# Operand tiles at other SBUF addresses, and reordered stage edges, in a hybrid two-layer decoder kernel

## The chip, the cores and the metric

One Trainium2 core of eight is used. The metric is the device time of one execution of the whole program in microseconds, median of several runs. The kernel before takes 1634.8 us (three runs: 1633.64, 1634.80, 1635.77).

The core has engines with a queue of instructions each: TensorE (PE, matrix products; PEld are its weight loads), VectorE (DVE), ScalarE (ACT), GpSimd (POOL), and SyncE (SP), which here only issues DMA transfers. Each engine works through its own queue in order; between engines order comes from semaphores. SBUF is the on-chip memory of 128 partitions, PSUM the accumulators of TensorE (eight banks of 128x512 fp32).

## The reference

A trunk of two layers on 512 tokens of width 1024, all in fp32:

```python
h = rms_norm(x, attn_norm[l])
proj = h @ w_in[l]                       # 5536 columns
gate_cols, mla_cols, rwkv_cols, conv_cols = split(proj)
o_a = mla_branch(mla_cols, ...)   @ mla_w_o[l]     # low-rank causal attention, 8 heads
o_b = rwkv7_branch(rwkv_cols, h, ...) @ rwkv_w_o[l]  # gated linear recurrence, 4 heads
o_c = short_conv_branch(conv_cols, ...) @ conv_w_o[l]
g = sigmoid(gate_cols).reshape(..., 3, 1024)
x = x + (g[0] * o_a + g[1] * o_b + g[2] * o_c) @ w_out[l]
h2 = rms_norm(x, mlp_norm[l])
x = x + square(relu(h2 @ w_up[l])) @ w_down[l]     # 1024 -> 4096 -> 1024
```

The recurrence of `rwkv7_branch` updates a 64x64 state per head and token; the kernel runs it in chunks of 64 tokens, each chunk as small matrix products.

## The kernel before, in words

**Layout.** Activations lie with channels on partitions and the 512 tokens along the free axis; a 128x512 tile is one slice of 128 channels. A dense product accumulates 128 output channels x 512 tokens in one PSUM bank over the slices k of its input.

**Three products for one.** Every fp32 operand of a dense product is split into hi (rounded) and lo (the rest), and each slice takes three matmuls with a 128x128 weight and a 128x512 moving operand: hi·act_hi (L269), hi·act_lo (L271), lo·act_hi (L273), in `gemm_steps`. Weights stream from DRAM in blocks of 128x512: `load_weights` issues the DMA into a `raw` tile (three buffers, L242), ScalarE casts it to `hi` (L243), VectorE subtracts to `lo` (L244), four buffers each. One block serves twelve matmuls. An input slice x is split in the same way into `xg` tiles: hi by ScalarE (L296), lo by VectorE (L297).

**Order.** TensorE's order is that of the program text (the matmuls stand under a manual schedule). The other engines' queues are ordered by a scheduler that simulates a timeline, with a few operations raised by `high_priority`. Because the recurrence and the attention are chains of small operations, the program weaves dense matmuls in between: `independent()` yields, matmul by matmul, the gate products and others that need only `xg`; `fill(n)` takes n of them, with the counts in the table `FC`.

**Stages of one layer.** (1) Norm of the input and five tiles of the input projection, one output tile after another; `normed_steps` (L309, sums of squares over channels) and `normed_spread` (L322–L324: four copies and transposes that spread the factor over partitions into `rstd`) are woven in; the first evacuations `col<-pg,rstd` wait for `rstd`. (2) The rest of the RWKV columns. (3) Chunk inputs: for each half j of the width, a chain on VectorE (cumulated decay L671, `k2` L673/L675, `a_` L676, `eC` L682, `ex` L685, `kk` L691, the four products into `ar` L696–L702), with exponentials on ScalarE (L679, L681), then `fill(FC["am"])` dense matmuls, then the products `pa,pb<-ar,ar` on TensorE (L714). (4) The recurrence over eight chunks; each has a group of 64x64 products at L842, in a loop over the output pair p and inside it over h. (5) Attention. (6) Merge: for each m of eight output tiles, load a gate tile `z` from DRAM (L1168), the product of `oa` (L1169, moving tile `prep`), gate and add (L561, L1170), split into hi and lo (L1174, L1175); then the product with `w_out` (moving tiles `ar` and `mix`), L1184. (7) MLP in four quarters q: eight up tiles (moving `xg`), then eight down tiles (192 matmuls) whose moving operands are the tiles `us` made from the up tiles: hi in `mix`, lo in `prep` for even q; hi in `ar`, lo in `mg` for odd q.

**Where the tiles lie.** All tiles come from one pool `sb`, which places tags in the order in which they first appear. Read from the compiled program, in bytes of each partition:

| tag | before | after |
|---|---|---|
| weights hi, lo | 29,792–46,175 | 7,264–23,647 |
| xg | 46,176–78,943 | 23,648–56,415 |
| prep | 101,472–122,271 | 56,416–76,895 |
| mix | 144,000–160,383 | 76,896–93,279 |
| ar | 162,464–178,847 | 93,280–109,663 |
| mg | 178,848–201,727 | 109,664–132,191 |
| raw | 23,648–29,791 | from 148,576 |

Of the kernel before, what the change touches and what calls it, by code (L numbers as in the profile page):

```python
# [16 lines left out]
F32R = mybir.dt.float32r  # L17
# [23 lines left out]
FC = {"ss": 9, "pk": 16, "am": 42, "tri0": 6, "tri1": 10, "join0": 22, "join1": 9, "join2": 8, "in1": 9, "py": 2,  # L41
# [16 lines left out]
def _blocks(inp, l):  # L58
# [3 lines left out]
    for t in RW_ORDER[:3]:  # L62
        out.append(_cols(w_in[:, r0 + t * P:r0 + (t + 1) * P]))
# [4 lines left out]
    out.append(_cols(ex))  # L68
# [98 lines left out]
def trunk(tc, w, wkv, wq, xin, pos, pp, sm, rg, out, sizes):  # L167
# [4 lines left out]
    const = es.enter_context(tc.tile_pool(name="const", bufs=1))  # L172
    sb = es.enter_context(tc.tile_pool(name="sb", bufs=1))
# [4 lines left out]
    BUFS = {"xg": 16, "mix": 8, "prep": 10, "am": 1, "ar": 4, "inv": 9, "tok": 2, "raw": 3, "hl": 4, "z": 2,  # L178
            "mg": 11, "col": 7, "g": 2, "a": 2, "b": 2, "c": 2}
    cnt = [0]  # L180

    def tl(tag, shape=(P, T), dt=F32, bufs=None):
        cnt[0] += 1
        if tag in ("prep", "mg") and tuple(shape) == (P, T):
            return sb.tile([P, 520 if tag == "prep" else T + 2], dt, tag=tag, name=f"{tag}_{cnt[0]}", bufs=BUFS[tag])[:, 0:T]
        return sb.tile(list(shape), dt, tag=tag, name=f"{tag}_{cnt[0]}", bufs=bufs or BUFS[tag])

# [99 lines left out]
    def split(tag, src, scale=None, tag_lo=None):  # L287

        hi = tl(tag, (P, T), F32R)
        lo = tl(tag_lo or tag, (P, T), F32R)  # L290
        if scale is None:
            A.copy(hi, src)
            V.tensor_tensor(out=lo, in0=src, in1=hi, op=ALU.subtract)
        else:
            last_split[:] = [
                A.activation(out=hi, in_=src, func=AF.Copy, scale=scale),  # L296
                V.scalar_tensor_tensor(out=lo, in0=src, scalar=scale, in1=hi, op0=ALU.mult, op1=ALU.subtract)]  # L297
        return hi, lo

# [192 lines left out]
    for l in range(NL):  # L492
        pr, dv, rgl = ppt[l], drv[l], rgt[l]
        sl = tl("sm", (P, 3 * RW), bufs=1)
        nc.sync.dma_start(out=sl, in_=sm[l])
# [67 lines left out]
        def independent():  # L563
# [103 lines left out]
        for j in range(2):  # L667
# [5 lines left out]
            V.tensor_scalar(out=k2, in0=a_, scalar1=dv[:, 6 + j:7 + j], scalar2=dv[:, 8 + j:9 + j],  # L673
                            op0=ALU.mult, op1=ALU.add)
            V.tensor_tensor(out=k2, in0=k2, in1=kt[j], op=ALU.mult)  # L675
            V.tensor_scalar(out=a_, in0=a_, scalar1=-0.5, scalar2=-0.5, op0=ALU.mult, op1=ALU.add)  # L676
            eW = tl("prep", (P, 8, C + 1))
# [7 lines left out]
            V.tensor_copy(ex, rs16v[:, :, j, :].unsqueeze(3).to_broadcast([P, NB, 2, C]))  # L685
# [20 lines left out]
            fill(FC["am"])  # L706
# [115 lines left out]
        def chunk_inputs(b):  # L822
# [17 lines left out]
            for p in range(2):  # L840
                for h, hs in enumerate(hss):
# [129 lines left out]
        def shared_key():  # L971
# [6 lines left out]
            kpr = tl("tok2", (P, NB, 32), bufs=1)  # L978
# [186 lines left out]
        for m in range(8):  # L1165
            wb = weights()
            z = tl("z")
            nc.sync.dma_start(out=z, in_=zd[l][:, m * T:(m + 1) * T])  # L1168
            run(branch_steps(z, wb, oa, 0, P, z))  # L1169
            (V if m > 5 else G).tensor_tensor(out=mg[m], in0=mg[m], in1=z, op=ALU.add)  # L1170
            if m % 2 == 0:
                mh = tl("ar", (P, 2, T), F32R)
            lo = tl("mix", (P, T), F32R)
            A.copy(mh[:, m % 2], mg[m])  # L1174
            V.tensor_tensor(out=lo, in0=mg[m], in1=mh[:, m % 2], op=ALU.subtract)  # L1175
            merged.append((mh[:, m % 2], lo))
# [17 lines left out]
        for q in range(4):  # L1194
            us = []
            for m in range(8):
# [49 lines left out]
```

## Time and profile before

| what | value |
|---|---|
| runs, median (lowest, highest) | 1634.8 us (1633.64, 1635.77) |
| profiled execution, its own time | 1636.34 us |
| its span, first to last instruction | 1634.6 us |
| TensorE busy | 1617.3 us, 99% |
| VectorE busy | 1016.8 us, 62% |
| ScalarE busy | 659.3 us, 40% |
| DMA | 156.79 MB, mean 96 GB/s |
| mean granted clock of TensorE | 0.998 |

A row of the timeline reads: start (us), duration (us), engine, line, operation, output<-inputs, shapes, count, and in brackets how long the engine sat idle before it and what released it. Matmuls are pipelined: the time that one occupies in the stream is the distance from its start to the next start, not its duration. In the view of windows a row is the stretch, its length, then for each engine the busy time with the number of instructions, then TensorE's granted clock (1.00 is full), the DMA engines' share and GB/s; asked for one engine, only that engine's column stands there.

### The profile page before, as it was taken

The page shows a single profiled execution, that of the slowest core. Times are in us where ns is not written, and L with a number is a line of the kernel's source. Part 1 is how long each engine was busy: PE and PEld are TensorE (multiplying, and loading weights), DVE is VectorE, ACT ScalarE, POOL GpSimd, SP SyncE. Part 2 cuts the span into 40 slices and gives each one's busy share as a digit, 9 for nine tenths or more (in the row PEclk, how much of TensorE's full clock was granted, in tenths as well). Part 3 has the DMA queues.
Part 4 walks back from the last instruction along what each step waited for, and adds up shares of the span by engine and source line. Part 5 has one row for each costly group of instructions (what it writes and reads, how often), then busy time and mean ns, then how long its engine had stood idle before and what let it go on. Part 6 is the DMA issues. An engine that isn't in the chain of part 4 may idle for free.

```text
span 1634.6 us, 22593 instructions
## 1 busy us (share of the span) xinstructions
PE 1617.3 (99%) x8126; PEld 1306.0 (80%) x8126; DVE 1016.8 (62%) x1988; ACT 659.3 (40%) x1457; POOL 185.8 (11%) x192
## 2 busy tenths in 40 slices
PE   8999999999999999999999999999999999999998
PEld 7878778877788888888887887887777888888887
DVE  7789577676754444544567886686766544444453
ACT  5332556454443232424333335654534433323241
POOL 1212024102100000000022121251120000000000
PEclk9999999999999999999999999999999999999999
DMA  5323322214323333333432243222143333333333
GB/s 163 95 73 108 110 66 80 82 46 129 123 91 97 97 97 95 95 95 97 141 98 78 79 127 92 63 72 73 51 146 113 92 95 97 97 97 96 93 96 103
DMA packets 85072, 156.79 MB, mean 96 GB/s; under 512 B 10080, under 2 KB 12384, under 8 KB 84448
## 3 DMA queue, kind: packets, MB, share of 16 engines
q1 hardware_dynamic: 84960, 155.35, 32.3%
q8 instruction: 64, 1.05, 0.3%
q14 instruction: 48, 0.39, 0.1%
HBM read 146.40 MB, written 8.91 MB: 95 GB/s over the span
## 4 chain that ended last, share of the span: by engine, by line
PE 93%; DVE 3%; DMA 2%; issue 1%; ACT 0%; SPq 0%; POOL 0%; DVEq 0%; ACTq 0%
PE pg L271 15%; PE pg L269 15%; PE pg L273 15%; PE pa L273 4%; PE pa L271 4%; PE pa L269 4%; PE pb L273 4%; PE pb L271 4%; PE pb L269 4%; PE pc L271 4%; PE pc L273 4%; PE pc L269 4%; PE pa L1115 2%; DMA z<-z_spill 1%; PE pc L1141 1%; DVE lo L244 1%
## 5 line engine op out<-in xcount | busy, mean ns | idle before, releaser
L243 ACT CAST hi<-raw 128x512 fp32r<-128x512 f32 (+1 forms) x499 | 307.1, 618 | 629.2 <-PE pg L271 255.6
L244 DVE TENSOR_TENSOR lo<-raw,hi 128x512 fp32r<-128x512 f32 (+1 forms) x499 | 358.2, 718 | 244.6 <-ACT hi L243 239.1
L269 PE MATMUL pg<-xg,hi 128*128 128x512 f32 x784 | 312.3, 398 | 2.9 <-ACT xg L296 2.2
L271 PE MATMUL pg<-xg,hi 128*128 128x512 f32 x784 | 313.8, 400 | 0.3 <-DVE xg L297 0.3
L273 PE MATMUL pg<-xg,lo 128*128 128x512 f32 x784 | 310.0, 395 | 0.0
L269 PEld LDWEIGHTS pg<-xg,hi 128*128 128x128 f32 x784 | 147.9, 189 | 39.3 <-issue 4.7
L271 PEld LDWEIGHTS pg<-xg,hi 128*128 128x128 f32 x784 | 148.0, 189 | 34.2 <-issue 5.8
L273 PEld LDWEIGHTS pg<-xg,lo 128*128 128x128 f32 x784 | 147.8, 189 | 31.6 <-issue 2.3
L303 POOL TENSOR_TENSOR t<-t,mhalf 128x4 f32<-128x4 f32 (+1 forms) x26 | 48.9, 1882 | 560.8 <-DVE t L314 536.7
L269 PE MATMUL pg<-ar,hi 128*128 128x512 f32 x192 | 75.7, 394 | 0.1
L273 PE MATMUL pg<-ar,lo 128*128 128x512 f32 x192 | 75.5, 393 | 0.0
L273 PE MATMUL pa<-xg,lo 128*128 128x512 f32 x160 | 62.6, 391 | 0.0
L269 PE MATMUL pa<-xg,hi 128*128 128x512 f32 x160 | 62.3, 390 | 0.0
L271 PE MATMUL pa<-xg,hi 128*128 128x512 f32 x160 | 62.3, 389 | 0.0
L271 PE MATMUL pg<-mix,hi 128*128 128x512 f32 x144 | 57.5, 399 | 1.3 <-DVE mix L1175 1.3
L273 PE MATMUL pb<-xg,lo 128*128 128x512 f32 x144 | 56.2, 390 | 0.0
L269 PE MATMUL pb<-xg,hi 128*128 128x512 f32 x144 | 56.1, 390 | 0.0
L271 PE MATMUL pb<-xg,hi 128*128 128x512 f32 x144 | 56.0, 389 | 0.0
L1119 ACT ACTIVATE inv<-pa,t 128x128 f32<-128x128 f32 (+3 forms) x64 | 33.7, 527 | 46.2 <-DVE t L1117 45.7
L271 PE MATMUL pg<-prep,hi 128*128 128x512 f32 x128 | 50.5, 394 | 0.0
L269 PE MATMUL pc<-xg,hi 128*128 128x512 f32 x128 | 50.0, 390 | 0.0
L273 PE MATMUL pc<-xg,lo 128*128 128x512 f32 x128 | 49.8, 389 | 0.0
(385 smaller groups left out, 3197.7 us busy)
## 6 DMA issues: line engine op xcount, KB each, us to landing
raw<-in_w_dram SPq DMA_DIRECT2D x493, 256.0 KB, 2.6
z_spill<-z SPq DMA_DIRECT2D x16, 256.0 KB, 3.1
z<-z_spill SPq DMA_DIRECT2D x16, 256.0 KB, 2.9
raw<-in_wq_dram SPq DMA_DIRECT2D x12, 192.0 KB, 2.3
am<-in_x_dram SPq DMA_DIRECT2D x8, 256.0 KB, 6.1
raw<-in_wkv_dram SPq DMA_DIRECT2D x8, 256.0 KB, 2.7
am<-in_x_dram SPq DMA_DIRECT2D x2, 1024.0 KB, 6.1
x_spill<-am SPq DMA_DIRECT2D x8, 256.0 KB, 2.9
```

Source lines behind the costliest of these rows:

```text
L243: A.copy(hi[:, c], raw[:, c])
L244: V.tensor_tensor(out=lo[:, c], in0=raw[:, c], in1=hi[:, c], op=ALU.subtract)
L269: mm(dst, hi[:, c0:c0 + P], ah, start=(k == 0), stop=False)
L271: mm(dst, hi[:, c0:c0 + P], al, start=False, stop=False)
L273: mm(dst, lo[:, c0:c0 + P], ah, start=False, stop=(k == n - 1))
L303: G.tensor_tensor(out=y, in0=v, in1=mhalf.to_broadcast([P, n]), op=ALU.pow)
L1115: mm(psc[:, 0:n], qT[hf][h // 2][0:HD, h % 2, b * P:n], kT[hf][h // 2][0:HD, h % 2, 0:n], start=True, stop=False)
L1119: A.activation(out=pe[:, 0:n], in_=psc[:, 0:n], func=AF.Exp, bias=nm[:, h:h + 1], accum_out=rsum[:, h:h + 1])
L1141: mm(po[halves[i], f], Vm[hf][kb // 2][:, kb % 2, 2 * f + i], pT[2 * f + i][:, kb * P:(kb + 1) * P], start=(kb == 0), stop=(kb == b))
```

## The change

1. A second pool `sbl`, allocated first, takes the tags hi, lo, xg, prep, mix, ar and mg, all with 2048 bytes per buffer (the padding to 520 and 514 columns is gone); the few odd-sized tiles go to `kql` and `rv`. The table above shows the addresses that result.
2. The first four tiles of the input projection (three RWKV tiles and the extra tile) are computed slice by slice: four accumulators are open, and for each k all four take their three matmuls. The host packs the weights accordingly, and the loads of x and of the weights alternate. `normed_steps` comes after all 96 matmuls, `normed_spread` inside the fifth tile.
3. `raw` has four buffers.
4. In the chunk chain, `k2`'s and `a_`'s scalings and the copies `eC` and `ex` move from VectorE to ScalarE, and `FC["am"]` becomes (50, 40) for j = 0, 1 instead of 42 for both.
5. The loop at L842 has h outside and p inside.
6. In the merge, `z` is loaded into `inv` (nine buffers) instead of `z` (two), and the last two additions and splits are raised in priority. `places` chooses the tiles of `merged` and of `us`: for m < 4 of even quarters `mix`, above it `prep`; for odd quarters `ar` and `mg`; for `merged`, `ar` and `mix`.

```diff
-FC = {"ss": 9, "pk": 16, "am": 42, ...
+FC = {"ss": 9, "pk": 16, "am": (50, 40), ...
...
+    sbl = es.enter_context(tc.tile_pool(name="sbl", bufs=1))
     sb = es.enter_context(tc.tile_pool(name="sb", bufs=1))
...
-    BUFS = {"xg": 16, ..., "raw": 3, "hl": 4, "z": 2,
+    BUFS = {"xg": 16, ..., "raw": 4, "hl": 4, "z": 2,
...
-        if tag in ("prep", "mg") and tuple(shape) == (P, T):
-            return sb.tile([P, 520 if tag == "prep" else T + 2], dt, tag=tag, ...)[:, 0:T]
-        return sb.tile(list(shape), dt, tag=tag, ...)
+        pool = sbl if tag in ("hi", "lo", "xg", "prep", "mix", "ar", "mg") else sb
+        return pool.tile(list(shape), dt, tag=tag, ...)
...
+    def places(m, tag):
+        if tag is None:
+            return tuple(tl("mix" if m < 4 else "prep", (P, T), F32R) for _ in range(2))
+        if m < 4:
+            both = tl("ar", (P, 2, T), F32R)
+            return both[:, 0], both[:, 1]
+        return tuple(tl(tag, (P, T), F32R) for _ in range(2))
+
+    def split_into(hl, src):
+        A.copy(hl[0], src)
+        V.tensor_tensor(out=hl[1], in0=src, in1=hl[0], op=ALU.subtract)
...
     for k in range(KD):
         nc.sync.dma_start(out=xt[:, k], in_=xin[:, k * T:(k + 1) * T])
-        if k in (0, 3):
-            ahead.append(load_weights(2))
-    ahead += [load_weights(2), load_weights()]
+        if k < 4:
+            ahead.append(load_weights(2 if k < 2 else 1))
...
-        pgs = []
-        at = 2 if l else 3
-        for i, pst in enumerate(("g", "g", "a", "b", "a")):
-            pgs.append(rwkv_gemm(pst, normed_steps if i == at else None))
-            if i == at:
+        pgs = [pt(pst) for pst in ("g", "g", "a", "b")]
+        for k, (ah, al) in enumerate(xg):
+            hi, lo = weights()
+            for t, pg in enumerate(pgs):
+                c = slice(t * P, (t + 1) * P)
+                mm(pg, hi[:, c], ah, start=(k == 0), stop=False)
+                mm(pg, hi[:, c], al, start=False, stop=False)
+                mm(pg, lo[:, c], ah, start=False, stop=(k == KD - 1))
+        for _ in normed_steps:
+            pass
+        pgs.append(pt("a"))
+        for i, _ in enumerate(gemm_steps(pgs[4], None, xg)):
+            if i == 14:
                 normed_spread()
...
-            V.tensor_scalar(out=k2, in0=a_, scalar1=dv[:, 6 + j:7 + j], scalar2=dv[:, 8 + j:9 + j],
-                            op0=ALU.mult, op1=ALU.add)
+            A.activation(out=k2, in_=a_, func=AF.Identity, scale=dv[:, 6 + j:7 + j], bias=dv[:, 8 + j:9 + j])
             V.tensor_tensor(out=k2, in0=k2, in1=kt[j], op=ALU.mult)
-            V.tensor_scalar(out=a_, in0=a_, scalar1=-0.5, scalar2=-0.5, op0=ALU.mult, op1=ALU.add)
+            A.activation(out=a_, in_=a_, func=AF.Copy, scale=-0.5, bias=-0.5)
...
-            V.tensor_copy(eC[:, j, :], eW[:, :, C])
+            A.copy(eC[:, j, :], eW[:, :, C])
...
-            V.tensor_copy(ex, rs16v[:, :, j, :].unsqueeze(3).to_broadcast([P, NB, 2, C]))
+            A.copy(ex, rs16v[:, :, j, :].unsqueeze(3).to_broadcast([P, NB, 2, C]))
...
-            fill(FC["am"])
+            fill(FC["am"][j])
...
-            for p in range(2):
-                for h, hs in enumerate(hss):
+            for h, hs in enumerate(hss):
+                for p in range(2):
                     mm(prs[p][halves[1 - p], hs], AM[halves[p], h, b, p, halves[1 - p]], uvs[p][halves[p], hs], ...)
...
-            z = tl("z")
+            z = tl("inv")
             nc.sync.dma_start(out=z, in_=zd[l][:, m * T:(m + 1) * T])
             run(branch_steps(z, wb, oa, 0, P, z))
-            (V if m > 5 else G).tensor_tensor(out=mg[m], in0=mg[m], in1=z, op=ALU.add)
-            ...
+            merged.append(places(m, "mix"))
+            with tc.high_priority() if m > 5 else nullcontext():
+                (V if m > 5 else G).tensor_tensor(out=mg[m], in0=mg[m], in1=z, op=ALU.add)
+                split_into(merged[m], mg[m])
...
-                if q % 2 == 0:
-                    us.append(split("mix", rl, tag_lo="prep"))
-                else:
-                    ...
+                us.append(places(m, "mg") if q % 2 else places(m, None))
+                split_into(us[m], rl)
```

**The start on TensorE.** The first dense matmuls of the program; `xg_138`, `xg_139` are hi and lo of slice k = 0, `xg_142`, `xg_143` those of k = 1, and `hi_99`, `hi_102` are weight blocks. Before:

```order
L215 MATMUL pc_81<-ident 128x128 x9
L269 MATMUL pg_323<-xg_138,hi_99 128x512
L271 MATMUL pg_323<-xg_139,hi_99 128x512
L273 MATMUL pg_323<-xg_138,lo_100 128x512
L269 MATMUL pg_323<-xg_142,hi_99 128x512
L271 MATMUL pg_323<-xg_143,hi_99 128x512
```

Of the change (the three matmuls of the loop stand at L544–L546 there):

```order
L544 MATMUL pg_321<-xg_138,hi_102 128x512
L545 MATMUL pg_321<-xg_139,hi_102 128x512
L546 MATMUL pg_321<-xg_138,lo_103 128x512
L544 MATMUL pg_322<-xg_138,hi_102 128x512
L545 MATMUL pg_322<-xg_139,hi_102 128x512
L546 MATMUL pg_322<-xg_138,lo_103 128x512
L544 MATMUL pa_323<-xg_138,hi_102 128x512
L545 MATMUL pa_323<-xg_139,hi_102 128x512
L546 MATMUL pa_323<-xg_138,lo_103 128x512
L544 MATMUL pb_324<-xg_138,hi_102 128x512
```

Slice k = 1 is needed after three matmuls before, after twelve now.

**The chunk chain on VectorE**, layer 0, up to the product `ar_812` that the L714 matmuls of j = 0 wait for (rows of j = 1 stand among them). Before:

```order
L685 COPY prep_923<-t_140_740 128x512
L244 TENSOR_TENSOR lo_935<-raw_933,hi_934 128x512
L675 TENSOR_TENSOR prep_914<-prep_914,mix_574 128x512
L676 TENSOR_SCALAR prep_756<-prep_756 128x512
L682 COPY eC_708<-prep_918 128x8
L700 TENSOR_TENSOR prep_809<-prep_809,prep_748 128x512
L732 SCALAR_TENSOR_TENSOR prep_762<-mix_522,pp_78,prep_762 128x512
L547 TENSOR_TENSOR col_847<-pg_796,rstd_322 128x512
L244 TENSOR_TENSOR lo_967<-raw_965,hi_966 128x512
L701 TENSOR_TENSOR ar_812<-prep_809,prep_760 128x4x128
```

Of the change:

```order
L724 TENSOR_TENSOR ar_812<-prep_762,prep_760 128x4x2x64
L697 TENSOR_TENSOR prep_931<-prep_931,mix_574 128x512
L722 TENSOR_TENSOR prep_809<-prep_809,prep_748 128x512
L246 TENSOR_TENSOR lo_891<-raw_889,hi_890 128x512
L754 SCALAR_TENSOR_TENSOR prep_762<-mix_522,pp_81,prep_762 128x512
L723 TENSOR_TENSOR ar_812<-prep_809,prep_760 128x4x128
L720 TENSOR_TENSOR ar_971<-mix_617,kql_935 128x4x2x64
L570 TENSOR_TENSOR col_847<-pg_796,rstd_320 128x512
```

L685, L676 and L682 are gone from this queue (L673, which stood four rows ahead of the first row shown, too), one `lo` (L244) fewer stands ahead of `ar_812`, and the evacuation `col_847` now stands behind it.

**The small products of a chunk on TensorE**; pb_1841/pb_1842 and pb_1847/pb_1848 are the accumulators of p = 0 and p = 1. Before:

```order
L842 MATMUL pb_1841<-uv_1822,am_758 64x64 x4
L842 MATMUL pb_1842<-uv_1823,am_758 64x64 x4
L923 MATMUL pa_1855<-rv_1851,prep_1643 64x64 x2
L923 MATMUL pa_1855<-rv_1851,prep_1644 64x64 x2
L269 MATMUL pg_1794<-xg_158,hi_1833 128x512
```

Of the change:

```order
L864 MATMUL pb_1847<-uv_1828,am_758 64x64
L864 MATMUL pb_1848<-uv_1829,am_758 64x64
L864 MATMUL pb_1847<-uv_1828,am_758 64x64
L864 MATMUL pb_1848<-uv_1829,am_758 64x64
L864 MATMUL pb_1847<-uv_1828,am_758 64x64
```

The eight products of a group alternate between the two halves of the array instead of running four and four.

More of the change, by code (lines that the diff above doesn't have):

```diff
@@ L61, in _blocks @@
     out = []
-    for t in RW_ORDER[:3]:
-        out.append(_cols(w_in[:, r0 + t * P:r0 + (t + 1) * P]))
+    first = [w_in[:, r0 + t * P:r0 + (t + 1) * P] for t in RW_ORDER[:3]]
     ex = np.zeros((D, P), w_in.dtype)
@@ L67, in _blocks @@
         ex[:, 32:64] = inp["rwkv_v1"][l - 1]
-    out.append(_cols(ex))
+    first.append(ex)
+    for k in range(KD):
+        out.append(np.concatenate([f[k * P:(k + 1) * P] for f in first], axis=1))
     for t in RW_ORDER[3:]:
@@ L176, in trunk @@
     dram = es.enter_context(tc.tile_pool(name="dram", bufs=1, space=bass.MemoryType.DRAM))
-    BUFS = {"xg": 16, "mix": 8, "prep": 10, "am": 1, "ar": 4, "inv": 9, "tok": 2, "raw": 3, "hl": 4, "z": 2,
-            "mg": 11, "col": 7, "g": 2, "a": 2, "b": 2, "c": 2}
+    BUFS = {"xg": 16, "mix": 8, "prep": 10, "am": 1, "ar": 4, "inv": 9, "tok": 2, "raw": 4, "hl": 4, "z": 2,
+            "mg": 11, "col": 7, "kql": 4, "g": 2, "a": 2, "b": 2, "c": 2}
     cnt = [0]
@@ L183, in tl @@
         cnt[0] += 1
-        if tag in ("prep", "mg") and tuple(shape) == (P, T):
-            return sb.tile([P, 520 if tag == "prep" else T + 2], dt, tag=tag, name=f"{tag}_{cnt[0]}", bufs=BUFS[tag])[:, 0:T]
-        return sb.tile(list(shape), dt, tag=tag, name=f"{tag}_{cnt[0]}", bufs=bufs or BUFS[tag])
+        pool = sbl if tag in ("hi", "lo", "xg", "prep", "mix", "ar", "mg") else sb
+        return pool.tile(list(shape), dt, tag=tag, name=f"{tag}_{cnt[0]}", bufs=bufs or BUFS[tag])
     def pt(tag, shape=(P, T)):
@@ L251, in load_kq @@
         nc.sync.dma_start(out=raw, in_=src)
-        hi = tl("prep", (P, 520), F32R)[:, 0:n]
-        lo = tl("kql", (P, WW), F32R, bufs=4)[:, 0:n]
+        hi = tl("prep", (P, T), F32R)[:, 0:n]
+        lo = tl("kql", (P, 520), F32R)[:, 0:n]
         A.copy(hi, raw)
@@ L426, in rounded @@
     def rounded(dst, src):
-        ti = tl("prep", (P, 520), I32)[:, 0:NR]
+        ti = tl("prep", (P, T), I32)[:, 0:NR]
         V.tensor_copy(ti, src)
@@ L493, in trunk @@
         pr, dv, rgl = ppt[l], drv[l], rgt[l]
-        sl = tl("sm", (P, 3 * RW), bufs=1)
-        nc.sync.dma_start(out=sl, in_=sm[l])
         def pcol(name, k=0, n=1):
@@ L524, in rwkv_cols @@
             mixed[t] = m_
-        pgs = []
-        at = 2 if l else 3
-        for i, pst in enumerate(("g", "g", "a", "b", "a")):
-            pgs.append(rwkv_gemm(pst, normed_steps if i == at else None))
-            if i == at:
+        pgs = [pt(pst) for pst in ("g", "g", "a", "b")]
[8 more added lines that the diff above has]
+            pass
+        sl = tl("sm", (P, 3 * RW), bufs=1)
+        nc.sync.dma_start(out=sl, in_=sm[l])
+        pgs.append(pt("a"))
+        for i, _ in enumerate(gemm_steps(pgs[4], None, xg)):
+            if i == 14:
                 normed_spread()
@@ L887, in code_split @@
             gcol = pcol("kva", t) if t < 2 else pcol("qa", t - 2)
-            hi = tl("prep", (P, 520), F32R)[:, 0:T]
+            hi = tl("prep", (P, T), F32R)
             A.activation(out=hi, in_=craw[t], func=AF.Copy, scale=gcol)
```

22 lines of the change are left out of this document (5 added, 17 removed).

## The prediction

> **What bounds the kernel now.** I read the page's engine shares, its chain of waits, then TensorE's waits, and then windows of 192 matmuls each.
>
> ```profile
> PE 1617.3 (99%) x8126; PEld 1306.0 (80%) x8126; DVE 1016.8 (62%) x1988; ACT 659.3 (40%) x1457; POOL 185.8 (11%) x192
> PE 93%; DVE 3%; DMA 2%; issue 1%; ACT 0%; SPq 0%; POOL 0%; DVEq 0%; ACTq 0%
> ...
> PE pg L269 <- ACT xg L296: 2.2, 1, 2.2
> PE pa L714 <- DVE prep L678: 2.1, 1, 2.1
> PE pa L714 <- DVE ar L701: 1.8, 1, 1.8
> ...
> PE pg L271 <- DVE mix L1175: 1.3, 2, 1.1
> ```
>
> TensorE carries the end: 99% busy, 93% of the chain. The change aims at these four waits, 7.4 us; the rest of a gain can only come from the pace of the matmuls. The pace is not the same everywhere. An even down quarter of the MLP, the up quarter behind it and the odd down quarter after that, 192 matmuls each (the count holds those that straddle the edges):
>
> ```profile
> 509.92:554.40 44.48, 44.48 (x193) 1.00 0.33 94
> 554.40:597.96 43.56, 43.56 (x193) 1.00 0.35 99
> 597.96:642.48 44.52, 44.52 (x194) 1.00 0.31 94
> ...
> 1208.05 0.39 PE L269 MATMUL pg<-prep,hi 128*128 128x512 f32 x1
> 1230.27 0.40 PE L273 MATMUL pg<-prep,lo 128*128 128x512 f32 x1
> ```
>
> At full clock in all three, no waits, nearly equal DMA: 44.50/192 = 231.8 ns a matmul in the down quarters against 43.56/192 = 226.9 ns in the up quarters, 4.9 ns apart. The down quarters move `mix`, `prep`, `ar` and `mg`, the up quarter `xg`. The last two rows are the first and last of 96 matmuls of the `oa` product, which move `prep` alone: 22.22/95 = 233.9 ns, so one region suffices for the slow pace. What sets `xg` apart in the program is that it lies lowest, up to byte 78,943; every slow operand starts at 101,472 or above. A distance, an alignment of the buffers, or the neighbouring weights would do as well: in the program before, the three go together.
>
> **The start.**
>
> ```profile
> 5.50:13.65 8.15, 5.71 (x13) 0.79 0.88 302
> 10.00:12.00 2.00, 1.87 (x4) 1.49 (x5) 2.00 (x6) 1.93 (x5) 0.00 (x0) 0.54 1.03 379
> 12.00:14.00 2.00, 2.00 (x7) 1.62 (x6) 2.00 (x5) 2.00 (x4) 0.00 (x0) 0.61 0.88 268
> ```
>
> Twelve matmuls fill the stretch to 13.65 us; at 226.9 ns they need 2.72 us, so 5.43 us are lost to x arriving slice by slice while each slice feeds three matmuls. Slice by slice with four accumulators, each slice (256 KB of x, 256 KB of weights; 512 KB at 302–379 GB/s is 1.4–1.7 us) feeds twelve, 2.72 us: the feed outruns the work from the second slice on. But the stretch also holds a lowered clock, which cost little while TensorE starved: 0.54 and 0.61 of full over two microseconds each, (0.46 + 0.39) × 2 = 1.7 us of work, if it comes again with TensorE busy. 5.43 − 1.7 leaves 3.7; the first two slices still ramp, each with a cast and a subtraction for x and for w, which I put at 0.7. I take **−3.0**; bounds −4.5 (the low clock falls away in part) and −1.0 (the weights' second transfer lands behind x).
>
> The spread of the norm factor now comes after 96 matmuls, on the fifth tile; the first three evacuations and so the PSUM banks g, g, a, b wait for it:
>
> ```profile
> 33.77 0.38 PE L323 MATMUL pc<-ident,tok 128*128 128x128 f32 x2
> 35.48 0.69 DVE L521 TENSOR_TENSOR col<-pg,rstd 128x512 f32<-128x512 f32 x1 [0.36 <-ACT rstd L324]
> ```
>
> From the first transpose to the first evacuation's end is 2.4 us, 10.6 matmuls of `xg`. The fifth tile has 24, of which ten follow step 14, and the sixth tile takes a g bank, free after that evacuation: cover and need are about equal, and the sums of squares stand just ahead. In both layers together I charge **+0.8** (0 to +2).
>
> **The chunk inputs.** In both layers TensorE waits for the products `ar`.
>
> ```profile
> 81.16 0.39 PE L269 MATMUL pg<-xg,hi 128*128 128x512 f32 x1
> 83.39 0.37 PE L714 MATMUL pa<-ar,ar 64*128 64x128 f32 x1 [1.84 <-DVE ar L701]
> 85.38 1.12 PE L734 MATMUL pc<-prep,bones 128*128 128x512 f32 x2
> 891.01 0.39 PE L269 MATMUL pg<-xg,hi 128*128 128x512 f32 x1
> 893.50 0.37 PE L714 MATMUL pa<-ar,ar 64*128 64x128 f32 x1 [2.11 <-DVE prep L678]
> 896.61 1.61 PE L734 MATMUL pc<-prep,bones 128*128 128x512 f32 x2
> ...
> 895.00:897.00 2.00, 2.00 (x17) 1.78 (x16) 2.00 (x5) 0.00 (x0) 0.55 (x1) 0.50 0.45 117
> ```
>
> Layer 0: 2.23 us from start to start where a matmul takes 0.23, so 2.0 lost. Layer 1: 2.49 − 0.23 = 2.26, and after the wait the clock is at half (0.50 in the last row): the products take 3.11 us against 1.99 in layer 0. Together 2.0 + 2.26 + 1.12 = 5.4 us.
>
> What VectorE loses per half is L673, L685, L676 and the small L682:
>
> ```profile
> 70.22 0.52 DVE L673 TENSOR_SCALAR prep<-prep,drv 128x512 f32<-128x512 f32 x1
> 70.68 0.42 DVE L685 COPY prep<-t 128x512 f32<-128x512 f32 x1
> ...
> 72.21 0.42 DVE L676 TENSOR_SCALAR prep<-prep 128x512 f32<-128x512 f32 x1
> ...
> 82.06 0.68 DVE L244 TENSOR_TENSOR lo<-raw,hi 128x512 fp32r<-128x512 f32 x1
> 82.66 0.68 DVE L701 TENSOR_TENSOR ar<-prep,prep 128x512 f32<-128x512 f32 x1
> ...
> 70.34 0.64 ACT L679 ACTIVATE prep<-prep 128x512 f32<-128x512 f32 x1 [0.54 <-DVE prep L671]
> ```
>
> The three 128x512 ones last 0.52, 0.42 and 0.42 with 0.46 from the first row's start to the second's, so they keep VectorE for some 0.9 of their duration: about 1.2 us, 2.4 for both halves, which both stand ahead of the first L701. One evacuation and one `lo` (0.6 start to start) fall behind it, another 1.2: `ar` is ready 3.6 us earlier. TensorE comes eight fill matmuls later (50 for 42), 8 × 0.227 = 1.8 us. 3.6 + 1.8 = 5.4 against waits of 2.0 and 2.26, so slack of some 3 us is left. The cost goes to ScalarE, 40% busy: two scalings of at most some 0.64 us, as its exponentials here take, ahead of the exponentials on which `ar` depends, which delays them by up to 1.3; the slack holds it. The eight fills come out of a pool that the end of the stage runs down anyway, and j = 1 gives two back. I take **−5.2**, bounds −5.4 and −3.0 (the clock of layer 1 falls all the same, and a part of a wait stays). If the cover fails, the wait returns on ScalarE's exponential and the term is near 0.
>
> **L842.**
>
> ```profile
> 187.79 0.96 PE L842 MATMUL pb<-uv,am 64*64 64x64 f32 x16
> 188.69 0.38 PE L225 MATMUL pa<-st,ar 128*128 128x128 f32 x1
> 187.85 0.43 DVE L944 TENSOR_TENSOR st<-st,ebd 128x256 f32<-128x256 f32 x1
> 83.61 0.27 PE L714 MATMUL pb<-ar,ar 64*128 64x128 f32 x1
> 83.72 0.27 PE L714 MATMUL pa<-ar,ar 64*128 64x128 f32 x1
> ```
>
> A group takes 0.89–0.9 us for sixteen records one behind the other. At L714 products on alternate halves of the array start together, a pair each 0.11. With 64 columns where those have 128, I estimate a pair at 0.07 to 0.08, eight pairs 0.62: 0.27 less per group, eight groups, −2.2. L225 behind it needs `st`, done at 188.28; it would now start at 188.42, so the cover is 0.14. I take **−2.0** (0, if they don't overlap, to −2.3).
>
> **The merge.** The waits for L1175 in the list are 1.3 us in both layers, and in layer 1 the first matmul of w_out starts 0.52 behind the last of `oa` (1230.27 above), 0.29 more than a matmul takes: 1.6.
>
> ```profile
> 421.78 0.69 DVE L561 SCALAR_TENSOR_TENSOR z<-z,pg 128x512 f32<-128x512 f32 x1 [1.49 <-DMA z<-z_spill]
> 1230.79 0.47 PE L269 MATMUL pg<-ar,hi 128*128 128x512 f32 x1
> ```
>
> VectorE sat 1.49 us for `z`, with two buffers; nine buffers load all eight early, and the last split no longer queues behind weights. On SP eight loads of 256 KB go in front of the weight loads, some 6 us at the 302–379 GB/s above; the weights have four raw and four cast blocks in stock, 2.72 us of work each, which covers it. I take **−1.4** (bounds 0 and −1.6). The fourth raw buffer costs and brings nothing: no wait for weights stands in the list.
>
> **The places.** 1,536 down matmuls (2 layers × 4 quarters × 192), 384 of w_out and 192 of `oa` move slow operands, 2,112 in all; 4.9 ns each is 10.3 us if all reach `xg`'s pace. But only `prep` (to 76,895) ends within the bytes where `xg` is fast now; it carries half the even quarters and `oa`, 384 + 192 = 576, 2.8 us. `mix` (76,896–93,279; 576 matmuls) lies in the gap that no trace shows, another 2.8. Most of `ar` and all of `mg` lie where `prep` is slow now. I take the middle of 2.8 and 5.6, **−4.2**; bounds 0 and −10.3.
>
> The Trainium skill, "SBUF — State Buffer", section "Who interferes with whom", says that TensorE never waits on anyone for SBUF. By that rule the place of an operand would not matter and this term is 0. The rows 44.48 against 43.56 show an effect of something, and the rule names nothing that would make it; it is the second case below.
>
> **Sum**, against the profiled execution of 1636.3 us: −3.0 + 0.8 − 5.2 − 2.0 − 1.4 − 4.2 = −15.0, 1621.3. That execution lies 1.5 us over the median of the runs, 1634.8; for the timed median I forecast 1620, rounded from 1619.8.
>
> **The rivals.**
> - *Forecast*, 1612–1626: **0.50**.
> - *The place does nothing*: the pace goes with what produces the operand or with its neighbours, 1619.8 + 4.2 = 1624.0. For it: the `oa` matmuls differ from the down ones, 233.9 against 231.8, though both move high tiles. **0.17**.
> - *All moved operands reach `xg`'s pace* (alignment, since all now sit on one stride): 10.3 instead of 4.2, 1613.7. **0.12**.
> - *The waits move*: `ar` then waits for ScalarE and the merge for weights behind `z`; the 5.2 and 1.4 are gone, 1626.4. Against it: ScalarE's 40%. **0.09**.
> - *Nothing comes of it*: start, chain and place each give back what they save; 1631.5 to 1638. **0.06**.
> - *Slower: `xg` loses its pace.* These rows hold the fast operand:
>
> ```profile
> L269 PE MATMUL pg<-xg,hi 128*128 128x512 f32 x784 | 312.3, 398 | 2.9 <-ACT xg L296 2.2
> L269 PE MATMUL pa<-xg,hi 128*128 128x512 f32 x160 | 62.3, 390 | 0.0
> L269 PE MATMUL pb<-xg,hi 128*128 128x512 f32 x144 | 56.1, 390 | 0.0
> L269 PE MATMUL pc<-xg,hi 128*128 128x512 f32 x128 | 50.0, 390 | 0.0
> ```
>
> Times three they are 3,648 matmuls, and `xg` moves to 23,648–56,415, where mostly none of it was; no row shows a dense operand below 46,176. At 4.9 ns it would cost 17.9 us. Without the gain of place the other terms are −10.8, so it decides from 60% of `xg` on; in full, −10.8 + 17.9 = +7.1, 1641.9. **0.06**.
>
> The range: 1609 to 1629 holds the first four cases but for their tails. Within 0.2% (3.3 us), which is about what can be told from no change, lies the fifth case and little of the fourth: faster 0.86, same 0.08, slower 0.06.
>
> **What would show it.** In the changed profile: the start without gaps from the third slice on and 96 matmuls done by some 28 to 30 us (right) or gaps for x or w (wrong); no wait at the `ar` products and full clock behind them in layer 1, or a wait there for an ACT row; L842 groups of about 0.62; no wait for `mix` at w_out; the down quarters at about 44.1 (even) and 44.5 (odd) with up quarters still at 43.56. Up quarters above 44 would make the whole prediction wrong, down quarters unchanged the place alone.

## The result, and the profile after

The changed kernel takes 1611.42 us (median of four runs, 1611.24 to 1611.63) against 1635.28 us before (1633.64 to 1636.31): ratio 0.9855, 95% interval 0.9838 to 0.9872. It is 23.9 us faster; 15 were forecast. One execution of all that are recorded here, of the version with the placement alone, took 7054.82 us at a mean granted clock of 0.217; no ratio includes it.

The engine shares, the chain's shares, and TensorE's waits of the changed kernel, which answer to the first rows of the prediction:

```profile
PE 1597.3 (99%) x8126; PEld 1301.9 (81%) x8126; DVE 1014.6 (63%) x1971; ACT 665.7 (41%) x1472; POOL 185.3 (12%) x192
PE 96%; DVE 2%; DMA 1%; ACT 0%; issue 0%; SPq 0%; DVEq 0%
...
PE pa L227 <- DVE st L966: 2.4, 3, 1.3
PE pc L217 <- POOL ident L203: 1.5, 1, 1.5
PE pc L338 <- DVE tok L337: 1.4, 4, 0.5
PE pa L945 <- ACT rv L868: 1.1, 2, 0.5
PE pg L271 <- DVE z L577: 0.7, 2, 0.4
PE pa L945 <- DVE rr L931: 0.6, 2, 0.4
```

The four waits that the change aimed at are gone from the list. Others have grown, above all for `st` in the recurrence (1.1 before) and for `tok` in the spread (0.8 before). TensorE's busy time fell by 20 us with the same 8126 instructions. That is not all pace: the rows of matmuls also stretch at half clock and cover a part of each wait (in the prediction's row 10.00:12.00 TensorE is 1.87 us busy with four matmuls). What is pace can be had from the starts: added up over all pairs of dense matmuls less than 300 ns apart, the excess over 226.67 ns (43.52/192) fell by 11.3 of the 24.7 us by which the span fell. Windows of TensorE, again an even down quarter, an up quarter, an odd down quarter, and as the fourth the `oa` product of layer 1:

```profile
500.51:544.03 43.52, 43.52 (x194) 1.00 0.34 96
544.03:587.55 43.52, 43.52 (x194) 1.00 0.34 99
587.55:631.07 43.52, 43.52 (x194) 1.00 0.34 98
1189.60:1211.35 21.75, 21.75 (x97) 1.00 0.46 155
```

All now run at 226.7 ns a matmul (43.52/192; 21.75/96 = 226.6), also the odd quarter, whose `mg` lies at 109,664–132,191, as high as the slow `prep` lay before.

Where the time went, by the start of the n-th dense matmul in both traces (5,952 in each; the numbers say by how much the changed kernel's lead over the kernel before grows within the stretch):

| stretch | gained there, us |
|---|---|
| first 96 matmuls, layer 0 | 5.4 |
| spread and rest of the fifth tile, layer 0 | −1.2 |
| to the end of the chunk inputs, layer 0 | 1.9 |
| recurrence and attention, layer 0 | 0.3 |
| `oa` and w_out, layer 0 | 3.0 |
| MLP, layer 0 | 4.1 |
| first five tiles, layer 1 | −0.2 |
| to the end of the chunk inputs, layer 1 | 3.8 |
| recurrence and attention, layer 1 | 1.0 |
| `oa` and w_out, layer 1 | 2.5 |
| MLP, layer 1 | 4.1 |

The first two rows have to be read together. The eight small matmuls of `normed_steps` stand ahead of the 96th dense matmul before the change and behind it now; they take 0.8 us beyond a matmul's pace (1.04 us from the dense matmul ahead of them to the one behind, 27.60 to 28.64, where 0.23 is usual). Of the 5.4 us that much only moved to the next stretch: the start itself gained 4.6, and the spread cost 0.4. Before, then of the changed kernel, the 96th dense matmul, the sums, and the wait in the spread:

```profile
27.83 0.95 PE L309 MATMUL pc<-ones,inv 128*128 128x1 f32 x8
33.54 0.39 PE L273 MATMUL pb<-xg,lo 128*128 128x512 f32 x1
34.36 0.47 PE L323 MATMUL pc<-ident,tok 128*128 128x128 f32 x2 [0.21 <-DVE tok L322]
...
28.13 0.39 PE L546 MATMUL pb<-xg,lo 128*128 128x512 f32 x1
28.36 0.94 PE L324 MATMUL pc<-ones,inv 128*128 128x1 f32 x8
33.58 0.46 PE L338 MATMUL pc<-ident,tok 128*128 128x128 f32 x2 [0.48 <-DVE tok L337]
```

At the start little starves (the first twelve dense matmuls take 3.56 us, 0.84 more than at full pace) and the clock does not fall (windows of the changed kernel: the first twelve dense matmuls, then the other 84; all engines, then the clock):

```profile
5.41:8.97 3.56, 3.39 (x13) 2.35 (x13) 2.99 (x7) 1.73 (x4) 0.00 (x0) 1.00 0.94 284
8.97:28.13 19.16, 19.11 (x85) 15.50 (x83) 18.70 (x56) 14.72 (x24) 0.00 (x0) 1.00 0.72 240
```

### The profile page after: what moved, and what is told of

Read it like the earlier page. It is cut to its first block, busy times and chain, and to the rows that moved or that the text cites. A ratio compares the mean times of both kernels' runs of the same rounds, so it can differ in the third digit from the quotient of the medians.

```text
span 1609.9 us, 22583 instructions
## 1 busy us (share of the span) xinstructions
PE 1597.3 (99%) x8126; PEld 1301.9 (81%) x8126; DVE 1014.6 (63%) x1971; ACT 665.7 (41%) x1472; POOL 185.3 (12%) x192
## 4 chain that ended last, share of the span: by engine, by line
PE 96%; DVE 2%; DMA 1%; ACT 0%; issue 0%; SPq 0%; DVEq 0%
PE pg L271 16%; PE pg L273 16%; PE pg L275 16%; PE pa L271 4%; PE pa L275 4%; PE pa L273 4%; PE pc L275 4%; PE pb L275 4%; PE pc L273 4%; PE pb L273 4%; PE pc L271 4%; PE pb L271 4%; PE pa L1137 2%; PE pc L1163 1%; PE pb L1151 1%; DMA raw<-in_wkv_dram 1%
## 5 line engine op out<-in xcount | busy, mean ns | idle before, releaser
L271 PE MATMUL pg<-xg,hi 128*128 128x512 f32 x752 | 299.0, 398 | 0.7 <-DVE z L577 0.7
L273 PE MATMUL pg<-xg,hi 128*128 128x512 f32 x752 | 299.0, 398 | 0.0
L275 PE MATMUL pg<-xg,lo 128*128 128x512 f32 x752 | 296.1, 394 | 0.0
L271 PEld LDWEIGHTS pg<-xg,hi 128*128 128x128 f32 x752 | 141.4, 188 | 35.2 <-issue 4.3
L273 PEld LDWEIGHTS pg<-xg,hi 128*128 128x128 f32 x752 | 141.5, 188 | 31.7 <-issue 5.2
L275 PEld LDWEIGHTS pg<-xg,lo 128*128 128x128 f32 x752 | 141.4, 188 | 29.2 <-issue 1.9
L271 PE MATMUL pa<-xg,hi 128*128 128x512 f32 x144 | 56.5, 392 | 0.0
L273 PE MATMUL pa<-xg,hi 128*128 128x512 f32 x144 | 56.1, 390 | 0.0
L271 PE MATMUL pg<-mix,hi 128*128 128x512 f32 x128 | 50.6, 395 | 0.0
L275 PE MATMUL pg<-mix,lo 128*128 128x512 f32 x128 | 50.3, 393 | 0.0
L271 PE MATMUL pc<-xg,hi 128*128 128x512 f32 x128 | 50.0, 391 | 0.0
L273 PE MATMUL pc<-xg,hi 128*128 128x512 f32 x128 | 49.8, 389 | 0.0
L273 PE MATMUL pb<-xg,hi 128*128 128x512 f32 x128 | 49.8, 389 | 0.0
L271 PE MATMUL pb<-xg,hi 128*128 128x512 f32 x128 | 49.8, 389 | 0.0
L631 POOL TENSOR_TENSOR mg<-mg,z 128x512 f32<-128x512 f32 x16 | 23.7, 1483 | 186.1 <-DVE z L584 145.4
```

Of the source, the lines that this page charges most:

```text
L271: mm(dst, hi[:, c0:c0 + P], ah, start=(k == 0), stop=False)
L273: mm(dst, hi[:, c0:c0 + P], al, start=False, stop=False)
L275: mm(dst, lo[:, c0:c0 + P], ah, start=False, stop=(k == n - 1))
L631: G.tensor_tensor(out=mg[m], in0=mg[m], in1=z, op=ALU.add)
```

## The experiments

All times in one place. "Before" is the kernel before on the same chip; spans are of the profiled executions (before 1634.6, changed 1609.9). Two profiled executions of the changed kernel, 1609.9 and 1610.8, lie 0.9 us apart, so no difference of two spans is surer than that.

| version | time, us | before, us | ratio, 95% interval | span, us |
|---|---|---|---|---|
| placement alone on before | 1627.6 | 1637.16 | 0.9948, 0.9932–0.9964 | 1625.9 |
| changed, pads 64 / 128 / 256 | 1623.73 | 1637.16 | one run | 1622.0 |
| changed, pads 32 / 512 / 1024 | 1630.15 | 1637.16 | one run | 1628.4 |
| changed, operands high | 1612.17 | 1637.16 | one run | 1610.5 |
| changed, `lo` 128 off | 1632.89 | 1636.53 | one run | 1631.2 |
| changed, old start | 1615.25 | 1636.13 | 0.9874, 0.9845–0.9902 | 1613.8 |
| changed, old chain and 42 fills | 1615.88 | 1636.13 | 0.9877, 0.9849–0.9906 | 1614.1 |
| changed, old loop at L842 | 1611.73 | 1636.13 | 0.9852, 0.9823–0.9881 | 1609.9 |
| changed, old `z` buffers and priority | 1615.25 | 1636.13 | 0.9874, 0.9845–0.9902 | 1613.4 |
| further version | 1610.15 | 1636.53 | 0.9839, 0.9823–0.9855 | 1608.2 |
| changed, again | 1611.82 | 1634.41 | 0.9859, 0.9843–0.9876 | 1610.8 |
| further version, again | 1610.61 | 1634.41 | 0.9852, 0.9837–0.9867 | 1609.0 |

### Is it the placement, and what of it?

Theory after the result: the pace hangs on how the moving operand's address stands to the weights' address, modulo some power of two; in the new pool every tag stands at 1120 modulo 2048. In the kernel before only `xg` shared this with the weights; `mix` stood at 640, `ar` at 672, and `prep` and `mg`, whose buffers stood 2080 bytes apart (20,800 bytes for ten, 22,880 for eleven in the table), had varying residues. Rivals: low addresses are fast (the prediction's reading), or it is enough that the moving operands agree with one another.

**Placement alone.** The edit on the kernel before (and the odd-sized tiles into `kql` and `rv`):

```diff
+    sbl = es.enter_context(tc.tile_pool(name="sbl", bufs=1))
     sb = es.enter_context(tc.tile_pool(name="sb", bufs=1))
...
-        if tag in ("prep", "mg") and tuple(shape) == (P, T):
-            return sb.tile([P, 520 if tag == "prep" else T + 2], ...)[:, 0:T]
+        pool = sbl if tag in ("hi", "lo", "xg", "prep", "mix", "ar", "mg") else sb
```

> The kernel before with the new pools alone (every operand tag in one pool of 2048-byte buffers; order, start, chain, L842, merge and the tags of merged and us as before). Theory P, the placement sets the pace of the dense matmuls: down quarters fall from 44.5 to 43.52 us, w_out and oa likewise, the sum over all dense intervals is 11.3 us less, and the waits at ar and mix stay: 1635.3 - 11 = 1624. Rival O, the pace comes from the new choice of tags for us and merged or from the order of the start: no change, 1635.

Its windows of an even down, an up and an odd down quarter, and its waits:

```profile
1316.65:1360.17 43.52, 43.52 (x193) 1.00 0.34 96
1360.17:1403.69 43.52, 43.52 (x193) 1.00 0.35 97
1403.69:1447.21 43.52, 43.52 (x193) 1.00 0.33 97
...
PE pa L714 <- DVE ar L701: 4.7, 2, 2.9
PE pg L271 <- DVE mix L1175: 2.3, 2, 1.3
```

It gives 9.5 us of the 23.9 by itself, by the medians; by the ratio it is 8.5, with an interval from 5.9 to 11.1. The excess over 226.67 ns, added up as above, fell from 14.6 to 3.6 us, 11.0 less; the span fell by 8.7, because TensorE now reaches `ar` and `mix` sooner and waits there longer: 4.7 us for `ar` (2.1 + 1.8 before) and 2.3 for `mix` (1.3 before). The rival that the tags of `us` or the order of the start make the pace is out: neither was changed.

**High.** The two pool lines exchanged:

```diff
-    sbl = es.enter_context(tc.tile_pool(name="sbl", bufs=1))
     sb = es.enter_context(tc.tile_pool(name="sb", bufs=1))
+    sbl = es.enter_context(tc.tile_pool(name="sbl", bufs=1))
```

> The changed kernel with the operand pool laid behind the other one, so that weights stand at 103,392 and the moving operands at 119,776 to 228,319, all with one offset modulo 2048 (992 where the changed kernel has 1120). Theory R and theory U: nothing changes, 1611, all quarters 43.52 us. Theory L, low addresses are fast: every dense operand is now where prep was slow, 1611 + 5,950 x 4.9 ns = 1640.

```profile
1301.15:1344.67 43.52, 43.52 (x193) 1.00 0.34 97
1344.67:1388.19 43.52, 43.52 (x193) 1.00 0.34 97
1388.19:1431.71 43.52, 43.52 (x193) 1.00 0.33 97
```

These windows are an even down, an up and an odd down quarter. With every operand above byte 103,000 the pace is the same and the time 1612.17. Theory L, the prediction's reading of the address, has fallen. So has an absolute residue of 1120; here it is 992 for all.

**Pads.** A tile that nothing uses is allocated ahead of the first buffer of a tag (three `raw` buffers instead of four make room):

```diff
+        if tag in PADS:   # first {xg: 64, prep: 64, ar: 128} bytes, then {xg: 32, prep: 480, ar: 512}
+            sbl.tile([P, PADS.pop(tag)], F32, tag="pad_" + tag, bufs=1)
         pool = sbl if tag in (...) else sb
```

> The changed kernel with three raw buffers and pads that move xg by 64 bytes against the weights, prep and mix by 128 bytes, ar and mg by 256 bytes; every tag stays uniform within itself. Theory R, the pace hangs on the offset between moving operand and weight modulo some power of two: the tags whose offset is no multiple of it go to 230-234 ns (up quarters 44.2-44.9 us where xg is hit); with a period of 512 all three are hit, 1611 + about 29 = 1640; with a period of 64 none. Theory U, uniform residues among the moving operands are enough: all stay at 226.7 ns, 1611. Theory L, low addresses: no change, 1611.

> As the run before, with xg moved by 32 bytes against the weights, prep and mix by 512, ar and mg by 1024. Theory R with a period of 64 to 512: xg alone is hit, up quarters 44.2 us or more and down quarters 43.52; 1611 + 3,600 x 4.9 ns = 1629. With a period of 2048: all are hit, 1640. Theories U and L: 1611, no quarter above 43.6 us.

The quarters even down (`mix`, `prep`), up (`xg`), odd down (`ar`, `mg`) of the first of the two, where these tags stand 128, 64 and 256 bytes off the weights:

```profile
1309.11:1353.74 44.63, 44.63 (x194) 1.00 0.34 95
1353.74:1397.70 43.96, 43.96 (x193) 1.00 0.33 96
1397.70:1441.23 43.53, 43.53 (x193) 1.00 0.33 96
```

And of the second, with offsets of 512, 32 and 1024 bytes:

```profile
1315.12:1358.67 43.55, 43.55 (x194) 1.00 0.34 98
1358.67:1403.47 44.80, 44.80 (x194) 1.00 0.32 94
1403.47:1447.03 43.56, 43.56 (x194) 1.00 0.36 97
```

Per matmul: 233.3 ns at 32 bytes off, 229.0 at 64, 232.4 at 128, and 226.7 to 226.9 at 256, 512 and 1024. Theory R holds, with a power of two that divides 256 but not 128, so 256 bytes; theory U falls, since each tag was uniform in itself. The up quarter, fast in every kernel so far, is the slow one as soon as `xg` is 32 bytes off.

How slow a matmul is does not follow from its own offset alone. In the kernel before, `mix` stood 32 bytes off the weights modulo 256 and `ar` 64, with tiles of varying offsets between them in each triple; both went at 231 to 232 ns from start to start, where the pads give 233.3 and 229.0. The figures by offset hold where all three matmuls of a triple share one.

**`lo` off.** 128 bytes ahead of `lo` and 128 more ahead of `xg`, by the same mechanism, so that only `lo` disagrees.

> The changed kernel with three raw buffers and 128 bytes of pad between the hi and the lo weights and 128 more behind lo: every moving operand stands a multiple of 256 bytes from hi, and 128 off lo. Theory K, TensorE's own weight load collides with its moving stream: only the stretch in which lo weights are loaded, beside the matmul ahead of lo x act_hi, is slow; one interval in three grows and the other two stay at 226.7 ns, up quarters 43.52 + 192/3 x (5 to 6 ns) = 43.9 us, 1611 + 10 = 1621. Rival M, the moving operands must agree with the tiles that ScalarE and VectorE write, or with hi alone: no interval grows, 1611. Rival N, any mismatch of any operand slows all: 44.5 us, 1640.

Its two windows, a down and an up quarter:

```profile
1315.89:1360.26 44.37, 44.37 (x193) 1.00 0.32 94
1360.26:1404.64 44.38, 44.38 (x194) 1.00 0.31 94
```

Mean distance from the start of a dense matmul to the next start, worked out from the trace by the place in the triple (the changed kernel has 227.1 to 227.4 in all three):

```
hi x act_hi   227.2 ns
hi x act_lo   232.4 ns   (lo is loaded beside it)
lo x act_hi   233.8 ns   (lo is in use, the next hi is loaded)
```

Theory K expected one slow interval of three; there are two, and the run cost 21 us instead of 10. Theory M, that `hi` alone matters, falls outright, and N, that all three slow down, too. So both an interval in which a disagreeing weight is loaded and one in which it is in use are slow. Why the second, when the weight loaded beside it agrees with what moves, is not settled.

### What the other parts are worth

The changed kernel was not run beside these four versions; the differences are taken against its 1611.42 us. It took 1611.82 us on the chip of the last two rows of the table.

**The old start** on the changed kernel (host packing, loads and loop as before).

```diff
-        pgs = [pt(pst) for pst in ("g", "g", "a", "b")]
-        for k, (ah, al) in enumerate(xg):
-            ...
+        for i, pst in enumerate(("g", "g", "a", "b", "a")):
+            pgs.append(rwkv_gemm(pst, normed_steps if i == at else None))
+            ...
```

> The changed kernel with the start of before (tile after tile, the old order of the loads, the spread after the fourth tile). By the two traces the new order won 5.4 us up to the 96th dense matmul of layer 0 and gave 1.2 back at the spread, and in layer 1 it only gives back about 1.2: so about 3 us slower than the changed kernel, some 1614.5. Theory C, the half clock of 10.2 to 13.6 us in the kernel before follows from TensorE's starving there: it comes back here. Rival, it strikes at random: no half clock, and the loss is 1.7 smaller.

Windows around the starvation of this version:

```profile
6.50:9.00 2.50, 0.37 (x2) 0.05 (x1) 1.05 (x2) 0.74 (x2) 0.00 (x0) 1.00 0.95 339
10.00:12.00 2.00, 2.00 (x5) 1.61 (x6) 2.00 (x5) 1.91 (x5) 0.00 (x0) 0.50 0.98 340
12.00:14.00 2.00, 2.00 (x8) 1.58 (x7) 2.00 (x4) 2.00 (x4) 0.00 (x0) 0.69 0.76 197
```

3.8 us slower than 1611.42, 3.9 by the spans: 5.8 at the 96th matmul, of which 1.2 are given back by the end of the fifth tile (0.8 of them the sums that only change places), 0.5 in the recurrence of layer 0, 0.2 in the first tiles of layer 1. The half clock is back with the starvation (0.50, where the changed kernel has 1.00): theory C.

**The old chain**: the four operations on VectorE, 42 fills for both halves.

```diff
-FC = {... "am": (50, 40)
+FC = {... "am": (42, 42)
-            A.activation(out=k2, in_=a_, func=AF.Identity, ...)
+            V.tensor_scalar(out=k2, in0=a_, ...)
...
```

> The changed kernel with the four operations of the chunk chain back on VectorE and 42 fill matmuls for both halves. Theory W, the waits of some 2 us for ar come back in both layers, and with them the half clock in layer 1 (1.1 to 1.6 us): 4 to 5.4 us slower than the changed kernel, 1615.5 to 1617. Rival, the earlier start of the stage and the other buffers had removed the wait already: under 1 us slower.

Its first wait in TensorE's list:

```profile
PE pa L737 <- DVE ar L724: 2.6, 2, 1.8
```

4.5 us slower (4.2 by the spans), theory W in size, not in all its parts: 1.9 us by the end of the chunk inputs of layer 0, 0.9 there in layer 1, no half clock, and the rest, 1.4, in the recurrence. That the shifted fills met the chunks differently there is likely, but not shown.

**The old loop at L842**, p outside and h inside.

> The changed kernel with p outside and h inside in the loop of small products. The forecast's sum: eight groups of 0.28, 2.0 to 2.2 us slower, 1613.5. Rival from the changed trace: in the third group of each layer TensorE waits for st (1.3 us in layer 1), in the first for the copy behind the products, so only the second and fourth group gain: four times 0.28, 1.1 us slower, and the waits for st shrink by 0.28 each.

1611.73 against 1611.42, and the spans are equal: the loop is worth nothing that can be told (the old one is 0.6 us ahead in layer 0 and 0.6 behind in layer 1). In the changed kernel a group of sixteen takes 0.61 (first two rows below), as forecast, against 0.89. The other rows show the third group of layer 1, by the timeline of TensorE and VectorE:

```profile
183.10 0.68 PE L864 MATMUL pb<-uv,am 64*64 64x64 f32 x16
183.71 0.49 PE L227 MATMUL pa<-st,ar 128*128 128x128 f32 x2
...
996.47 0.41 DVE L965 TENSOR_TENSOR st<-pa,st 128x256 f32<-128x256 f32 x1
996.80 0.68 DVE L246 TENSOR_TENSOR lo<-raw,hi 128x512 fp32r<-128x512 f32 x1
997.40 0.73 DVE L902 TENSOR_SCALAR mix<-pc,pp 128x128 f32<-128x128 f32 x2
998.04 0.42 DVE L966 TENSOR_TENSOR st<-st,ebd 128x256 f32<-128x256 f32 x1
998.60 0.57 PE L227 MATMUL pa<-st,ar 128*128 128x128 f32 x3 [1.26 <-DVE st L966]
```

Between the two halves of the `st` update VectorE's queue now holds a weight split and the scalings of `mix`; before, only the scalings stood there. The shorter group only waits longer: 2.4 us for `st` in all, against 1.7 with the old loop.

**The old merge**: `z` in its own two buffers, no raised priority.

```diff
-            z = tl("inv")
+            z = tl("z")
...
-            with tc.high_priority() if m > 5 else nullcontext():
+            if True:
```

> The changed kernel with z loaded into its two z buffers and without the raised priority of the last two splits. Theory: the stalls at the first matmuls of w_out come back, 1.2 us in layer 0 and 0.3 to 0.9 in layer 1, 1.5 to 2.0 us slower. Rival: the new tiles of merged and the faster oa product leave the last split in time; under 0.5 us.

The wait at w_out in layer 1 of this version:

```profile
1219.19 0.50 PE L273 MATMUL pg<-mix,hi 128*128 128x512 f32 x1 [1.01 <-DVE mix L313]
```

3.8 us slower (3.5 by the spans): 1.5 in layer 0 and 2.3 in layer 1, more than the waits of the kernel before added up to, because the `oa` product ahead of it is faster now (21.75 us where it took some 22.4) and outruns the two `z` buffers as well. Buffers and priority were undone together, so neither has a price of its own.

Undone or done alone, by the spans: placement 8.7, start 3.9, chain 4.2, merge 3.5, loop 0. That is 20.3 of 24.7; the other 4.4 us belong to no part alone. Placement on its own gives 2.3 us of its pace back, most of it in waits for `ar` (+0.8) and `mix` (+1.0) that the other parts remove. The tiles chosen by `places` and the fourth `raw` buffer were never undone by themselves.

### A further version

`ar` is ready 3.3 us (layer 0) and 2.3 us (layer 1) before TensorE comes for it in the changed kernel, and the waits left are for `st` and `tok`.

```diff
-FC = {... "am": (50, 40), ... "pr": 3
+FC = {... "am": (38, 40), ... "pr": 7
...
-            if i == 14:
+            if i == 20:
                 normed_spread()
...
-            rwkv_cols(t, rwkv_gemm())
+            rwkv_cols(t, rwkv_gemm("b" if t == RW_ORDER[4] else "g"))
```

> The changed kernel, with 38 fill matmuls instead of 50 ahead of the first ar products (there ar is ready 3.2 to 3.8 us before TensorE comes), the twelve given to the stretches between the state product and the next group (pr 7 for 3), the spread of the norm after step 20 of the fifth tile, and the sixth tile in the free b bank. Theory: no new wait at ar, the waits for st (2.4 us) and for tok (1.4 us) shrink by 2 to 3.5 us together, 1608 to 1609.5. Rival: the shifted fills put other evacuations into the chain of the chunks and the wait comes back elsewhere, 1610.5 to 1613.

> The changed kernel itself, on one chip with the version of the last row, to set the two beside each other: 1611.2 to 1612.2.

> The version with 38 fill matmuls, pr 7, the later spread and the sixth tile in the b bank. If the traces' 1.7 us between the two spans is the version's own: 1.3 to 1.9 us below the changed kernel, with ranges of all runs apart. If it was the chip: under 0.7 us, ranges overlapping.

1610.15 first; then on one chip 1610.61 (1610.52 to 1610.72) beside the changed kernel's 1611.82 (1611.63 to 1612.48): 1.2 us faster, with the ranges apart, where 2 to 3.5 were expected at first and 1.3 to 1.9 for the second time. The waits for `st` went from 2.4 us out of the list and those for `tok` from 1.4 to 0.8, but others grew, for `z` from 0.7 to 1.1 (waits of the further version's second profile; the 0.7 for `lo` stands in the changed kernel's second profile too):

```profile
PE pa L945 <- ACT rv L868: 1.2, 2, 0.6
PE pg L271 <- DVE z L577: 1.1, 2, 0.6
PE pc L338 <- DVE tok L337: 0.8, 4, 0.2
PE pg L546 <- DVE lo L246: 0.7, 2, 0.5
PE pa L227 <- DVE t L893: 0.5, 2, 0.3
```

## Why the prediction was right, and where it was not

The sign and the range (1609 to 1629) held, the forecast of 1620 was 8.6 us too high. 1611.4 lies below the 1612 to 1626 of the forecast's own case; the case that came nearest is the third, 1613.7, which had 0.12. That the range held is owed to its width, and in part to luck: start, merge and place each gave more than was charged, and the loop's −2.0 came to nothing. Step by step:

- **The places: the failed step.** The prediction saw the two paces rightly and put them down to the height of the address; by that, only `prep` and half of the gap became fast, −4.2. The runs show the offset between weight and moving operand modulo 256 bytes instead, so that all 2,112 slow matmuls reached the fast pace: 8.2 us in the MLP alone, 8.7 net and 11.0 in the intervals by the placement alone. That is the third case, alignment, priced at 10.3 and given 0.12. The prediction had named alignment as an equal reading of the same rows and still priced by height; the table of addresses, in which all these tags share one residue after the change, was the place to weigh the two. Why the offset acts as it does is not shown.
- **The place does nothing** (1624): fallen. Placement alone is worth 8.5 to 9.5 us, with an interval that excludes zero. The Trainium skill, "SBUF — State Buffer", section "Who interferes with whom", says that TensorE never waits on anyone. Read as a rule about other engines it is not touched by these runs; but the place of TensorE's own two operands matters all the same, 232.4 ns at 128 bytes off against 226.7.
- **The slower rival** (`xg` loses its pace at its new place) did not happen, but its mechanism exists: 32 bytes of pad make `xg` slow, 44.80 us a quarter.
- **The start**: −3.0 forecast; by the traces −4.6 (5.4 without the 0.8 for the sums), by undoing −5.0 (5.8 without them). The mis-sized term is the 1.7 us charged for a half clock that would come again; it follows from the starving and went with it. The 0.7 for the ramp was about right (0.84).
- **The spread**: +0.8 forecast for both layers, 0.4 + 0.2 measured, within the bounds. The wait for `tok` grew from 0.8 to 1.4 us: 14 steps are too few for the chain behind the sums of squares.
- **Chunk inputs**: −5.2 forecast, 1.9 + 3.8 in the traces; undone alone 4.2. Right in kind; the 5.7 lies a little beyond the bound of 5.4. The slack of some 3 us came out as 3.3 and 2.3. The eight more fills (1.8 us) were not needed for it, and with twelve fewer than the changed kernel has (2.7 us) the further version waits 0.3 us there once.
- **L842**: the group's 0.62 came true (0.61), the −2.0 did not. The cover of 0.14 us was named and taken as enough; what failed is the assumption that VectorE's queue around `st` stays as it was.
- **Merge**: −1.4 forecast; undone alone 3.5. The waits were counted at the old pace of `oa`; with the faster pace two `z` buffers and the old priority would have cost more, as the 2.3 us of waits for `mix` with the placement alone also show.
- **The waits move** (0.09): not to ScalarE's exponentials and not to the weights, as that case had it, but to `st` (+1.3 us), `tok` (+0.6), and the copies `rv` and `rr` (+0.6 each).

## What to carry to other kernels

From this one kernel: when one group of matmuls runs a few per cent slower than another of the same shape at full clock and without waits, compare the SBUF addresses of moving operand and weights modulo 256 bytes before looking elsewhere, and give all matmul operands buffers of a multiple of 256 bytes in one pool; padding a tile by a few columns can break this for it and for every tag behind it. Price a removed wait together with the pace that comes with it, since a faster TensorE arrives earlier at every other wait. And before shortening work that stands ahead of a wait, look at what the other engine's queue holds between it and its release.

## What the runs showed of the hardware that was not expected

- A 128x512 matmul follows the one before at 226.7 to 226.9 ns when its moving operand stands a multiple of 256 bytes from the weights, and at 229.0, 232.4 and 233.3 ns with 64, 128 and 32 bytes off modulo 256. The fast pace is the same at both heights tried, with moving operands from byte 23,648 and from 119,776.
- The half clock follows a starved TensorE. Over all traces taken, where TensorE had gaps from one start to the next of 2.50, 2.59, 2.66, 2.83 and 3.30 us, the granted clock fell to a half 0.7 to 1.5 us after the gap's end and stayed there for 3.4 us; behind eight gaps of 1.65 to 2.23 us it did not fall. The row of the longest, in the version with the placement alone, behind its wait for `ar` in layer 1:

```profile
892.00:894.00 2.00, 2.00 (x4) 0.87 (x4) 1.27 (x3) 0.00 (x0) 0.00 (x0) 0.50 0.14 52
```

So a gap of 2.2 us cost its own length, and one of 2.5 or more also a stretch of half speed. These are traces of versions of this one kernel; no run varied the gap by itself, and where between 2.23 and 2.50 us the border lies, or whether the gap's length alone decides, is not shown.
